# Key products, decay matrices and substitutions of a gated-delta layer moved among its input projections

## The chip, the cores and the metric

The kernel runs on one core of a Trainium2 chip. The time is the device time of one execution in microseconds (us); of several runs the median is given. The engines are TensorE (PE in the profile), VectorE (DVE), ScalarE (ACT), GpSimd (POOL) and SyncE (SP). Each takes its own instructions in a fixed order; a DMA is issued by one of them and moves its data beside them.

## The reference, cut to what matters

Two layers work on 16 meta tokens and 1024 tokens of width 1024, in float32. A layer is a norm, an input projection to 28 blocks of 128 columns, a mixer, an output projection and a feed-forward part. One half of the mixer is a gated delta rule with 4 heads of 128, run forwards and backwards over the sequence:

```python
decay_mat = jnp.exp(jnp.where(incl, G[..., :, None] - G[..., None, :], -jnp.inf))
M = jnp.where(strict, jnp.einsum('bnhid,bnhjd->bnhij', kb, k) * decay_mat, 0.0)
A = M + jnp.eye(CHUNK, dtype=M.dtype)
u = lax.linalg.triangular_solve(A, vb, left_side=True, lower=True, unit_diagonal=True)
w = lax.linalg.triangular_solve(A, kb * jnp.exp(G)[..., None], left_side=True, lower=True, unit_diagonal=True)
attn = jnp.einsum('bnhid,bnhjd->bnhij', q, k) * decay_mat
def step(S, inp):
    v_new = u_c - jnp.einsum('bhcd,bhde->bhce', w_c, S)
    o = jnp.einsum('bhcd,bhde->bhce', qd_c, S) + jnp.einsum('bhij,bhje->bhie', a_c, v_new)
    S = S * gl_c[..., None, None] + jnp.einsum('bhcd,bhce->bhde', kd_c, v_new)
```

k and q are the l2-normalised outputs of a three-tap convolution and a SiLU, G is the running sum of the log decay. The other half of the mixer is a gated short convolution over the remaining columns.

## The kernel before, in words

Activations lie with channels on partitions and the 1040 positions along the free axis. **Dense work** (`dense`, L139) multiplies one block of 128 output columns in fp32r with a split of both operands into a high and a low part: high x high, high x low, low x high (L150, L151, L152), 8 blocks of 128 inputs each, in three column chunks of about 347. ACT writes the high part of a weight (`whi`, L123), POOL the low part (`wlo`, L124); for the first three of the late projections DVE does that (`lov`). An evacuation on DVE multiplies the finished accumulator by the norm (L270). There are three accumulator banks (`pacc`), one bank `pa`, two `pf` and two `pb`.

The 28 projections of a layer go in this order: four k tiles, four q tiles, four v tiles, then 16 for the short convolution and the gate z. Each k, q or v tile gets a convolution (L283, L284) and a SiLU. Sums of squares give the l2 norm (`normalise`); its reciprocal is broadcast through DRAM and multiplied in (L392).

The delta rule goes in 9 chunks (the first of 16 positions, eight of 128) and two directions d. For a chunk the kernel forms K K and K Q products for four heads (L538, L539), loads a row of gate sums (`gr`, from the DRAM tile `gd`), adds a mask on POOL (L550) and takes exponentials on ACT (L548, L552). DVE writes the query side to `aq`, which goes to DRAM (`aqd`; L549, L556), and the key side to P (L560), one tile of 128 x 4160 for each direction. The matrices in P are inverted: first all 32x32 blocks on the diagonal by **substitution**, 31 steps of two vector instructions (L603 multiplies, L604 subtracts), on DVE for d = 0 and on POOL for d = 1; then **merges** on PE to 64x64 and 128x128 blocks (L627 to L653). The chunk of 16 is inverted apart by small instructions on POOL (L572, L573), the meta inversion. The **scan** then takes 9 steps in each direction. A step is a chain: PE (L700), DVE (L703), PE with P (L706), ACT (L710, L713), PE (L717), DVE for the state (L740), beside output products on PE (L731, L732). When both directions have reached a chunk it is finalised (`finalize`, L759 to L771) into O.

The output projection has two halves. The y half, from the short convolution, is dense work without need of the scan. The o half needs O split into a high and a low part (`oh`, `ol`; L827, L828), and these two tiles have the buffers of the two P: they can be written only when the scan has read P for the last time.

What sets the order is a priority list: a scheduler takes, engine by engine, the ready instruction with the lowest number, and the result is a fixed order for each engine. Code written first has lower numbers, unless it sets its own: the merges run at `base-20000+1000d`, the scan at `base-17000` and on, while dense work from the v tiles onwards is put at `base+1000000` (the variable `mmp`) and so fills gaps.

## Time and profile before

| | |
|---|---|
| median of 3 runs | 2680.13 us (2670.06 to 2682.99) |
| the profiled execution | 2667.47 us, span 2665.7 us |
| mean granted clock of TensorE | 0.983 |
| PE busy | 2563.4 us, 96% |
| DVE, ACT, POOL busy | 56%, 39%, 44% |
| DMA | 301.03 MB, mean 113 GB/s |

The profile is one execution; its sums are compared with its own 2667.47 us. A busy PE need not run at full speed: the granted clock is given in a row of its own, in tenths for each fortieth of the span, or as a fraction in a window. "A <- B" in a wait names who waited and for which tile of which line. Line numbers in the profile are those of the kernel before; in the changed kernel most lines after L100 are shifted (L150 to L152 become L152 to L154, the substitution is L506 and L507, the merges to 128x128 are L554 and L556, and the lines of the scan rise by 23).

### The profile page before, as it was taken

To read this page: it belongs to the slowest core of one execution; us is meant where nothing else is said; L and a number is where in the kernel's file an instruction comes from. 1 tells how busy PE (TensorE), PEld (TensorE's weight loads), DVE (VectorE), ACT (ScalarE), POOL (GpSimd) and SP (SyncE) were. 2 spreads that over 40 slices of the span, in tenths; PEclk is the share of its full clock that TensorE was granted. 3 is DMA by queue.
4 is the path that set the end of the run, shared out by engine and by line. 5 is a ranking of instruction groups with operands and counts; after the bars stand their busy time and mean duration, and the time that the engine had idled before them with its cause. 6 is when DMAs were issued, how large, how long until landed. Compare 5 with 4: busy or idle time off the path is not lost. (4 is left out here: it accounts for less than half of the span.)

```text
span 2665.7 us, 43982 instructions
## 1 busy us (share of the span) xinstructions
PE 2563.4 (96%) x17242; PEld 2346.7 (88%) x17242; DVE 1502.8 (56%) x2258; ACT 1032.8 (39%) x1932; POOL 1185.1 (44%) x922
## 2 busy tenths in 40 slices
PE   8998899999999999999999989999989999999997
PEld 7898899998999999999998977898877888887886
DVE  7369713548766566522353688135587766754216
ACT  5466334535333333321244662535343333332224
POOL 4136611224766666533221346112367666663342
PEclk9999889999999999999999999999999999999998
DMA  3246135634312222532222461356332222225321
GB/s 118 98 148 201 49 103 185 193 105 135 104 60 84 80 73 76 198 111 65 76 92 86 125 229 50 125 179 230 99 124 93 68 82 77 87 88 185 93 81 64
DMA packets 163491, 301.03 MB, mean 113 GB/s; under 512 B 20352, under 2 KB 57140, under 8 KB 163284
## 3 DMA queue, kind: packets, MB, share of 16 engines
q1 hardware_dynamic: 163284, 298.23, 34.2%
q8 instruction: 135, 2.21, 0.4%
q14 instruction: 72, 0.59, 0.1%
HBM read 222.99 MB, written 75.18 MB: 112 GB/s over the span
## 5 line engine op out<-in xcount | busy, mean ns | idle before, releaser
L124 POOL TENSOR_TENSOR wlo<-raw,whi 128x512 fp32r<-128x512 f32 x236 | 285.8, 1214 | 927.9 <-ACT whi L123 812.1
L150 PE MATMUL pacc<-a,whi 128*128 128x346 f32 (+2 forms) x1031 | 350.0, 342 | 10.6 <-ACT whi L123 6.1
L152 PE MATMUL pacc<-a,wlo 128*128 128x346 f32 (+2 forms) x1031 | 351.0, 342 | 6.8 <-DVE wlo L124 6.7
L123 ACT ACTIVATE whi<-raw 128x512 fp32r<-128x512 f32 (+2 forms) x264 | 151.7, 578 | 478.9 <-PE pacc L151 300.6
L151 PE MATMUL pacc<-a,whi 128*128 128x346 f32 (+2 forms) x916 | 313.2, 342 | 1.8 <-DVE a L799 1.7
L152 PE MATMUL pacc<-b,wlo 128*128 128x346 f32 (+2 forms) x882 | 303.3, 345 | 8.2 <-DVE wlo L124 8.2
L150 PE MATMUL pacc<-b,whi 128*128 128x346 f32 (+2 forms) x882 | 305.5, 347 | 4.2 <-ACT whi L123 2.1
L151 PE MATMUL pacc<-b,whi 128*128 128x346 f32 (+2 forms) x776 | 268.6, 347 | 0.7 <-DVE b L799 0.6
L150 PEld LDWEIGHTS pacc<-a,whi 128*128 128x128 f32 x1031 | 199.0, 194 | 21.7 <-ACT whi L123 6.5
L152 PEld LDWEIGHTS pacc<-a,wlo 128*128 128x128 f32 x1031 | 199.7, 194 | 16.5 <-DVE wlo L124 8.0
L151 PEld LDWEIGHTS pacc<-a,whi 128*128 128x128 f32 x916 | 177.3, 194 | 10.6 <-DVE a L799 2.0
L150 PEld LDWEIGHTS pacc<-b,whi 128*128 128x128 f32 x882 | 168.2, 191 | 20.1 <-issue 4.2
L152 PEld LDWEIGHTS pacc<-b,wlo 128*128 128x128 f32 x882 | 168.1, 191 | 19.2 <-DVE wlo L124 9.5
L942 POOL TENSOR_TENSOR wlo<-rw,whi 128x512 fp32r<-128x512 f32 x92 | 135.5, 1475 | 71.2 <-ACT whi L941 65.6
L151 PEld LDWEIGHTS pacc<-b,whi 128*128 128x128 f32 x776 | 147.9, 191 | 11.2 <-DVE b L799 1.6
L942 POOL TENSOR_TENSOR a<-rw,a 128x512 fp32r<-128x512 f32 x64 | 107.1, 1676 | 66.5 <-ACT a L941 66.4
L942 POOL TENSOR_TENSOR b<-rw,b 128x512 fp32r<-128x512 f32 x64 | 90.5, 1418 | 83.9 <-ACT b L941 52.3
L804 DVE TENSOR_TENSOR a<-pacc,a 128x346 f32<-128x346 f32 (+2 forms) x116 | 57.7, 500 | 108.3 <-PE pacc L152 107.1
L941 ACT ACTIVATE whi<-rw 128x512 fp32r<-128x512 f32 x92 | 58.0, 632 | 140.1 <-DVE rw L1015 72.5
L804 DVE TENSOR_TENSOR b<-pacc,b 128x512 f32<-128x512 f32 (+1 forms) x88 | 52.6, 599 | 99.2 <-PE pacc L152 98.9
L1011 DVE TENSOR_TENSOR rw<-rw,rw 128x512 f32<-128x512 f32 x44 | 68.5, 1556 | 49.3 <-POOL wlo L942 31.0
L1016 DVE TENSOR_TENSOR rw<-raw,rw 128x512 f32<-128x512 f32 x44 | 95.3, 2165 | 1.2
(822 smaller groups left out, 7504.3 us busy)
## 6 DMA issues: line engine op xcount, KB each, us to landing
raw<-in_w_in SPq DMA_DIRECT2D x112, 256.0 KB
raw<-in_w_gu SPq DMA_DIRECT2D x104, 256.0 KB
rw<-in_w_gu SPq DMA_DIRECT2D x88, 256.0 KB
aqd<-aq SPq DMA_DIRECT2D x32, 512.0 KB
rec<-aqd SPq DMA_DIRECT2D x62, 256.0 KB
rec<-vkd SPq DMA_DIRECT2D x61, 256.0 KB
raw<-in_w_dn SPq DMA_DIRECT2D x60, 256.0 KB
raw<-in_w_out SPq DMA_DIRECT2D x48, 256.0 KB
```

Source lines behind the costliest of these rows:

```text
L123: act(out=hi, in_=raw[:, 0:kk, :], func=AF.Copy)
L124: (tt if lov[0] else ptt)(out=lo, in0=raw[:, 0:kk, :], in1=hi.bitcast(F32), op=ALU.subtract)
L150: mm(ps[:, :n], wh, xh[:, n0:n1], start=(k == 0), stop=False)
L151: mm(ps[:, :n], wh, xl[:, n0:n1], start=False, stop=False)
L152: mm(ps[:, :n], wl, xh[:, n0:n1], start=False, stop=(k == K - 1))
L804: tt(out=hr[m][:, n0:n1], in0=ps, in1=hr[m][:, n0:n1], op=ALU.add)
L941: act(out=hi, in_=src, func=AF.Copy)
L942: ptt(out=lo, in0=src, in1=hi.bitcast(F32), op=ALU.subtract)
L1011: tt(out=s1t, in0=A21, in1=A22, op=ALU.add)
L1016: tt(out=A21, in0=A11, in1=A21, op=ALU.subtract)
```

## The change

The computation stays as it is; its place in the code, two engines and several transfers differ.

- `gates` is built after the third k tile (it was after the seventh of the eight k and q tiles), and its PSUM tiles come from bank `b`, not `a`.
- `normalise` sums squares into four column groups of 260, takes root and reciprocal in place, and issues its stores and broadcast loads from POOL's queue; the broadcast rows land in small tiles, not in a buffer of P.
- `chunks_p`, after the second q tile, does the key half of each chunk: K K products in one bank `b` (priority `base-25000`), mask on POOL, exponentials, P. The decay matrix is also stored to a new DRAM tile `dtd`. Loads and stores go through ACT's queue. The meta inversion gets priority `base+400000`.
- `invert(0)` is called after the q norm, `invert(1)` after the second v tile. Both use DVE and one scratch tile.
- `chunks_a`, after the v tiles, does the query half: K Q products, a second load of the gate rows and a load of the decay matrix (ACT's queue), `aq` and its store.
- The stores of k and v to `vkd` go through ACT's queue; the meta rows of v are stored tile by tile.

The core of the diff (the projection loops, which only move, are left out):

```diff
+    adma = nc.scalar.dma_start
+    qdma = nc.gpsimd.dma_start
...
-        def normalise(dst, l2, r, tag):
+        def normalise(dst, l2, r):
...
-            flat = rnd[r:r + 4].rearrange("a (b c) -> (a b) c", c=40)
-            r104 = row(Y[1] + "f")[0:104, 0:40]
-            dma(r104, flat)
-            nc.vector.reciprocal(out=r104, in_=r104)
-            dma(flat, r104)
-            bc = big(tag)
+            r4 = row(Y[1] + "f")[:, 0:260]
+            act(out=r4, in_=l2[:, 0:260], func=AF.Sqrt, scale=scale, bias=bias)
+            nc.vector.reciprocal(out=r4, in_=r4)
             for h in range(H):
-                dma(bc[:, h, :], rnd[r + h].partition_broadcast(128))
-                tt(out=dst[:, h, :], in0=dst[:, h, :], in1=bc[:, h, :], op=ALU.mult)
+                qdma(rnd[r + h].rearrange("(a c) -> a c", a=4), r4.rearrange("(a b) c -> a b c", b=32)[:, h, :])
+            for h in range(H):
+                bc = c4k("bc")
+                qdma(bc, rnd[r + h].partition_broadcast(128))
+                tt(out=dst[:, h, :], in0=dst[:, h, :], in1=bc, op=ALU.mult)
...
+        def chunks_p():
...
+            for c in range(9):
+                n, s0 = span(c)
+                kk = bank("b").rearrange("p (h i) -> p h i", h=4)
+                def products():
+                    for h in range(H):
+                        mm(kk[0:n, h, 0:n], KTt[:, h, s0:s0 + n], KTt[:, h, s0:s0 + n], start=True, stop=True)
+                at_base(-25000 + 10 * c, products)
+                for d in (dirs0 if c == 0 else (0, 1)):
+                    pn += 1
+                    gr, dt_ = pts[pn % 4], pts[4 + pn % 4]
+                    adma(gr[0:n, :, 0:n], gd[36 * d + 4 * c:36 * d + 4 * c + 4, 0:n].partition_broadcast(n))
+                    ptt(out=gr[0:n, :, 0:n], in0=gr[0:n, :, 0:n], in1=off[0:n, d, 0:n].unsqueeze(1).to_broadcast([n, 4, n]), op=ALU.add)
+                    for h in range(H):
+                        act(out=dt_[0:n, h, 0:n], in_=gr[0:n, h, 0:n], func=AF.Exp, scale=-1.0, bias=negG[0:n, d, c, h:h + 1])
+                    adma(dtd[c, d].rearrange("p (h i) -> p h i", h=4)[0:n, :, 0:n], dt_[0:n, :, 0:n])
+                    for h in range(H):
+                        dst = P0[d][:, h, :] if c == 0 else Pv[d][:, (c - 1) * 4 + h, :]
+                        stt(out=dst, in0=kk[0:n, h, 0:n], scalar=beta[0:n, d, c, h:h + 1], in1=dt_[0:n, h, 0:n], op0=ALU.mult, op1=ALU.mult)
...
+        def chunks_a():
+            for c in range(9):
+                n, s0 = span(c)
+                qk = bank("b").rearrange("p (h i) -> p h i", h=4)
                 for h in range(H):
+                    mm(qk[0:n, h, 0:n], KTt[:, h, s0:s0 + n], QT[:, h, s0:s0 + n], start=True, stop=True)
+                for d in (dirs0 if c == 0 else (0, 1)):
...
+                        eg = t2k("eg")
+                        adma(eg[:, :, 0:n], gd[36 * d + 4 * c:36 * d + 4 * c + 4, 0:n].partition_broadcast(128))
+                        act(out=eg[:, :, 0:n], in_=eg[:, :, 0:n], func=AF.Exp, scale=-1.0)
+                        tt(out=qd0 if c == 0 else qd, in0=QT[:, :, s0:s0 + n], in1=eg[:, :, 0:n], op=ALU.mult)
+                    dt_ = t2k("dt")
+                    adma(dt_[0:n, :, 0:n], dtd[c, d].rearrange("p (h i) -> p h i", h=4)[0:n, :, 0:n])
+                    tt(out=at0[d] if c == 0 else at, in0=qk[0:n, :, 0:n], in1=dt_[0:n, :, 0:n], op=ALU.mult)
+                    if c > 0:
+                        dma(aqd[c, d].rearrange("p a b -> p (a b)"), aq[:, 0:1024])
...
-                itt(out=Tm[:, i0:i1, a0:a1], in0=W[:, i0:i1, j:j + 1].to_broadcast(sh), in1=Xi[:, j:j + 1, a0:a1].to_broadcast(sh), op=ALU.mult)
-                itt(out=Xi[:, i0:i1, a0:a1], in0=Xi[:, i0:i1, a0:a1], in1=Tm[:, i0:i1, a0:a1], op=ALU.subtract)
+                tt(out=Tm[:, i0:i1, a0:a1], in0=W[:, i0:i1, j:j + 1].to_broadcast(sh), in1=Xi[:, j:j + 1, a0:a1].to_broadcast(sh), op=ALU.mult)
+                tt(out=Xi[:, i0:i1, a0:a1], in0=Xi[:, i0:i1, a0:a1], in1=Tm[:, i0:i1, a0:a1], op=ALU.subtract)
...
+            if pos == 2:
+                beta, g, negG, negE, gl, bkd = gates()
+            if pos == 3:
+                normalise(KTt, l2, 4)
+            if pos == 5:
+                for c in range(9):
+                    k_out(c)
+                chunks_p()
+        normalise(QT, l2, 0)
+        invert(0)
...
+            if i == 1:
+                invert(1)
+        chunks_a()
```

Three places show what the scheduler makes of it in layer 0. The second direction's substitution is the first: POOL before, where L550 is the mask of a chunk, L502 a product of the short convolution, and `b_418` the scratch tile of d = 1.

```order
L550 TENSOR_TENSOR ptm_3158<-ptm_3158,off 128x512
L502 TENSOR_TENSOR b_231_1841<-b_231_1841,b_232_1845 128x1040
L603 TENSOR_TENSOR b_418_3604<-b_418_3604 128x31
L604 TENSOR_TENSOR b_418_3604<-b_418_3604 128x31
L603 TENSOR_TENSOR b_418_3604<-b_418_3604 128x30x2
L604 TENSOR_TENSOR b_418_3604<-b_418_3604 128x30x2
```

And DVE now, where L126 is the low part of a weight, L272 an evacuation and `b_220` the scratch tile of d = 1:

```order
L272 TENSOR_TENSOR b_351_3060<-pacc_3073,rstd_81 128x348
L500 STREAM_TRANSPOSE b_220_2087<-b_220_2087 128x1024
L506 TENSOR_TENSOR b_220_2087<-b_220_2087 128x31
L272 TENSOR_TENSOR b_351_3060<-pacc_3099,rstd_81 128x346
L507 TENSOR_TENSOR b_220_2087<-b_220_2087 128x31
L506 TENSOR_TENSOR b_220_2087<-b_220_2087 128x30x2
L507 TENSOR_TENSOR b_220_2087<-b_220_2087 128x30x2
L506 TENSOR_TENSOR b_220_2087<-b_220_2087 128x29x3
L507 TENSOR_TENSOR b_220_2087<-b_220_2087 128x29x3
L506 TENSOR_TENSOR b_220_2087<-b_220_2087 128x28x4
L507 TENSOR_TENSOR b_220_2087<-b_220_2087 128x28x4
L126 TENSOR_TENSOR wlo_3161<-raw_3162,whi_3160 128x512
```

The substitution of d = 1 has moved from POOL to DVE and shares that queue with evacuations and low parts of weights.

The second place is PE at the merges of 64x64 blocks, L651 and L653 before (`pf`, `pb` are banks, `P_3149` and `P_3150` the matrices of d = 0 and d = 1, L627 a 32x32 merge; `x8` means eight instructions):

```order
L152 MATMUL pacc_2470<-a_1_72,wlo_2407 128x346
L627 MATMUL pb_4106<-b_418_3604,P_3150 32x32 x3
L653 MATMUL pf_3878<-P_3149,b_417_3603 64x64 x8
L651 MATMUL pf_3897<-b_417_3603,P_3149 64x64 x8
L627 MATMUL pb_4106<-b_418_3604,P_3150 32x32 x13
L653 MATMUL pf_3898<-P_3149,b_417_3603 64x64 x8
L651 MATMUL pf_3917<-b_417_3603,P_3149 64x64 x8
L627 MATMUL pb_4106<-b_418_3604,P_3150 32x32 x13
L653 MATMUL pf_3918<-P_3149,b_417_3603 64x64 x8
L653 MATMUL pf_3937<-P_3149,b_417_3603 64x64 x8
L627 MATMUL pb_4106<-b_418_3604,P_3150 32x32 x3
L150 MATMUL pacc_2470<-a_1_72,whi_2406 128x346
```

The same merges of d = 0 on PE now, as L554 and L556 (`P_1002` is the matrix of d = 0):

```order
L154 MATMUL pacc_3004<-a_3_74,wlo_2973 128x346
L556 MATMUL pf_1807<-P_1002,b_179_1539 64x64 x8
L554 MATMUL pf_1826<-b_179_1539,P_1002 64x64 x8
L152 MATMUL pacc_3004<-a_3_74,whi_2972 128x346
L153 MATMUL pacc_3004<-a_5_76,whi_2972 128x346
L154 MATMUL pacc_3004<-a_3_74,wlo_2973 128x346
L152 MATMUL pacc_3004<-a_3_74,whi_2972 128x346
L153 MATMUL pacc_3004<-a_6_77,whi_2972 128x346
```

The merges of the two directions stood together without dense work between them; now those of one direction stand alone, two groups at a time between runs of dense matmuls.

The third place is PE at the last read of P. Before, L706 is that read in the last step but one of d = 1, L770 a transpose of a finalise, and the rest is the dense work of an input projection, with the y half still to come:

```order
L151 MATMUL pacc_3123<-a_2_73,whi_3059 128x346
L706 MATMUL pb_4286<-vv_4282,P_3150 128x128 x4
L770 MATMUL pa_4944<-ident,b3f_4287 128x128 x4
L152 MATMUL pacc_3123<-a_1_72,wlo_3060 128x346
L150 MATMUL pacc_3123<-a_1_72,whi_3059 128x346
L151 MATMUL pacc_3123<-a_2_73,whi_3059 128x346
```

Now L729 is that read, L740 the state product, L754 and L755 the output products, L793 the transpose; the row after the last of these belongs to the next step, and the next dense rows are those of the o half:

```order
L153 MATMUL pacc_5614<-a3f_5229,whi_5580 128x346
L154 MATMUL pacc_5614<-a_521_5214,wlo_5581 128x346
L729 MATMUL pb_4373<-vv_4369,P_1003 128x128 x4
L793 MATMUL pa_5031<-ident,b3f_4374 128x128 x4
L740 MATMUL pb_4372<-vv_4369,rec_4364 128x128 x4
L754 MATMUL pb_4373<-S_4367,rec_4364 128x128
L755 MATMUL pb_4373<-vv_4369,rec_4364 128x128
```

The last read of P has moved from the last input projections to behind the last matmul of the y half.

More of the change, by code (lines that the diff above doesn't have):

```diff
@@ L658, in trunk @@
             at_prio(sub_end)
+        for pos, i in enumerate((4, 5, 6, 7, 0, 1, 2, 3)):
+            hh = pos % 4
+            if hh == 0:
+                l2, squares = None, []
+            t = trow()
+            late = pos < (2, 1)[l]
+            inproj(i, to_row_late(t) if late else to_row(t), pfirst if l == 0 and pos == 1 else None)
+            if late:
+                tt(out=t, in0=t, in1=rstd, op=ALU.mult)
+            dst = (QT if i < 4 else KTt)[:, hh, :]
+            conv(t, dst, P_CV + 3 * i)
+            act(out=dst, in_=dst, func=AF.Silu)
+            act(out=t, in_=dst, func=AF.Square)
+            squares.append((hh, t))
+            if l > 0 or pos > 0:
+                if l2 is None:
+                    l2 = bank("f")
+                for (q, sq_) in squares:
+                    for j, (n0, n1) in enumerate([(260 * j, 260 * j + 260) for j in range(4)]):
+                        mm(l2[32 * j:32 * j + 32, :n1 - n0], sel[:, 3 - q:35 - q], sq_[:, n0:n1], start=(q == 0), stop=(q == 3), skip_group_check=True)
+                squares = []
+            if pos == 2:
[6 more added lines that the diff above has]
+                chunks_p()
@@ new lines, in trunk, with z_tile, low @@
+        normalise(QT, l2, 0)
+        invert(0)
+        mmp[0] = base + 1000000
+        def z_tile(m):
+            t = trow()
+            inproj(12 + m, to_row(t), chunks=ochunks)
+            t = t[:, o0:L]
+            act(out=t, in_=t, func=AF.Silu)
+            nc.gpsimd.tensor_scalar(out=t, in0=t, scalar1=pcol(P_DN), scalar2=1.0, op0=ALU.mult, op1=ALU.mult)
+            dma(szd[m][:, o0:L], t)
+        def low(f):
+            here = tc.cur_priority
+            at_prio(mmp[0])
+            f()
+            mmp[0] = tc.cur_priority
+            at_prio(here)
@@ new lines, in v_store @@
+        def v_store(i, v):
+            for c0 in (0, 1, 5):
+                ps = pa()
+                if c0 == 0:
+                    low(lambda: nc.tensor.transpose(ps[0:16, 0:128], v[:, 0:16], ident))
+                    vm = wp.tile([128, WK, 128], F32, tag="raw", bufs=2, name=nm("vm"))[0:16, 0, :]
+                    nc.vector.tensor_copy(vm, ps[0:16, 0:128])
+                    dma(vkd[0, 0:16, 0, i * 128:(i + 1) * 128], vm)
+                else:
+                    vt = v[:, 16 + 128 * (c0 - 1):16 + 128 * (c0 + 3)]
+                    for c in range(4):
+                        low(lambda: nc.tensor.transpose(ps[:, c * 128:(c + 1) * 128], vt[:, 128 * c:128 * c + 128], ident))
+                    act(out=vt, in_=ps, func=AF.Copy)
+                    adma(vkd[c0:c0 + 4, :, 0, i * 128:(i + 1) * 128].rearrange("c p e -> p c e"), vt.rearrange("p (c e) -> p c e", c=4))
@@ new lines, in trunk, with sc_tile, times, f @@
+        v = None
+        for i in range(4):
+            t = trow()
+            inproj(8 + i, to_row(t))
+            if i > 0:
+                v_store(i - 1, v)
+            v = trow() if i % 2 == 0 else row(Y[1] + "f")
+            conv(t, v, P_CV + 3 * (8 + i))
+            act(out=v, in_=v, func=AF.Silu)
+            if i == 1:
+                invert(1)
+        chunks_a()
+        def sc_tile(i, then=None):
+            t0 = trow()
+            inproj(16 + 3 * i, to_row(t0))
+            if then is not None:
+                then()
+            ptt(out=t0, in0=t0, in1=rstd, op=ALU.mult)
+            def times(t):
+                def f(ps, n0, n1):
+                    tt(out=t[:, n0:n1], in0=ps, in1=t[:, n0:n1], op=ALU.mult)
+                return f
+            inproj(17 + 3 * i, times(t0))
+            t2 = trow()
+            conv(t0, t2, P_SC + 3 * i)
+            if i < 3:
+                t1 = trow()
+                inproj(18 + 3 * i, to_row(t1), chunks=ochunks)
+                ptt(out=t2[:, o0:L], in0=t2[:, o0:L], in1=t1[:, o0:L], op=ALU.mult)
+                dma(yd[i][:, o0:L], t2[:, o0:L])
+            else:
+                ptt(out=t2, in0=t2, in1=rstd, op=ALU.mult)
+                inproj(18 + 3 * i, times(t2), chunks=ochunks)
+            return t2
@@ L661, in trunk @@
+        y3 = None
+        for j, q in enumerate((0, 4, 1, 5, 6, 2, 7, 3)):
+            lov[0] = j < 3
+            if q < 4:
+                y3 = sc_tile(q, (lambda: v_store(3, v)) if j == 0 else None)
+            else:
+                z_tile(q - 4)
+        lov[0] = False
+        mmp[0] = None
+        top = tc.cur_priority
         rec = sb.tile([128, 4 * L], F32, tag=Y[0][2], name=nm("rec"))
```

215 lines of the change are left out of this document (45 added, 170 removed).

## The prediction

> **What bounds the kernel now.** I read the page first (busy shares and the clock row), then windows of 40 us over the part of each layer that the change touches, then the waits of PE there, then the groups of the instructions that move. Three rows of the page:
>
> ```profile
> PE 2563.4 (96%) x17242; PEld 2346.7 (88%) x17242; DVE 1502.8 (56%) x2258; ACT 1032.8 (39%) x1932; POOL 1185.1 (44%) x922
> PEclk9999889999999999999999999999999999999998
> q1 hardware_dynamic: 163284, 298.23, 34.2%
> ```
>
> PE is the bound at 96%, so a change that adds no matmul can only win back PE's idle time and time at a lowered clock, and can lose by adding to either. The windows show where both lie: busy us of PE, PEld, DVE, ACT and POOL, then the granted clock, the share of the DMA engines and GB/s. The first five rows are layer 0, the last four layer 1.
>
> ```profile
> 160.00:200.00 40.00, 37.15 (x255) 34.60 (x254) 28.28 (x64) 26.29 (x55) 20.30 (x33) 1.00 0.68 216
> 200.00:240.00 40.00, 34.28 (x230) 33.51 (x230) 37.55 (x83) 26.67 (x61) 31.89 (x48) 0.96 0.68 225
> 240.00:280.00 40.00, 35.59 (x210) 34.44 (x209) 36.22 (x65) 15.12 (x19) 21.68 (x28) 0.96 0.38 129
> 280.00:320.00 40.00, 34.43 (x335) 33.10 (x334) 31.66 (x50) 11.40 (x15) 28.62 (x43) 0.91 0.14 47
> 320.00:360.00 40.00, 38.65 (x579) 35.90 (x578) 8.85 (x11) 17.82 (x27) 3.52 (x3) 0.67 0.12 40
> ...
> 1520.00:1560.00 40.00, 34.01 (x232) 31.86 (x231) 32.05 (x80) 29.72 (x64) 26.21 (x41) 1.00 0.71 226
> 1560.00:1600.00 40.00, 35.34 (x176) 30.79 (x175) 38.10 (x78) 23.46 (x45) 15.54 (x16) 0.92 0.60 205
> 1600.00:1640.00 40.00, 34.08 (x177) 31.14 (x176) 38.73 (x58) 6.28 (x9) 34.76 (x46) 0.93 0.16 49
> 1640.00:1680.00 40.00, 38.99 (x635) 31.21 (x633) 19.89 (x27) 22.15 (x31) 13.92 (x18) 0.99 0.17 59
> ```
>
> In layer 0, PE idles 2.9 + 5.7 + 4.4 + 5.6 + 1.4 = 19.9 us, with DVE nearly full; and 0.04, 0.04, 0.09 and 0.33 of four windows of 40 us are lost to the clock, 20.0 us. In layer 1 it is 6.0 + 4.7 + 5.9 + 1.0 = 17.6 us idle and 6.4 us of clock. So 64 us in all can be won here. The large clock loss is the stretch of the 64x64 merges, where PE counts as fully busy at half speed; the last row is from the first scan steps, among dense work again:
>
> ```profile
> 340.00:345.00 5.00, 5.00 (x31) 4.08 (x30) 0.52 (x1) 0.59 (x1) 0.00 (x0) 0.50 0.00 0
> 350.00:355.00 5.00, 5.00 (x70) 4.82 (x68) 0.00 (x0) 1.18 (x2) 0.00 (x0) 0.50 0.00 0
> ...
> 375.00:380.00 5.00, 5.00 (x57) 4.48 (x54) 1.12 (x4) 1.78 (x3) 0.00 (x0) 1.00 0.15 50
> ```
>
> The largest waits of PE in 160 to 365 us name DVE and ACT:
>
> ```profile
> PE pacc L152 <- DVE wlo L124: 6.7, 3, 4.2
> PE pa L463 <- ACT b L471: 4.4, 1, 4.4
> PE pb L538 <- DVE P L560: 2.9, 3, 1.3
> ```
>
> No DMA is among them, although the DMA share is 0.68 there.
>
> **The substitutions.** Both directions ran side by side, one on DVE, one on POOL (busy us, mean ns):
>
> ```profile
> L603 DVE TENSOR_TENSOR b<-b 128x31 f32<-128x31 f32 (+15 forms) x31 | 17.0, 547 | 0.8
> L604 DVE TENSOR_TENSOR b<-b 128x31 f32<-128x31 f32 (+15 forms) x31 | 16.8, 542 | 0.7
> L604 POOL TENSOR_TENSOR b<-b 128x31 f32<-128x31 f32 (+15 forms) x31 | 19.7, 637 | 2.2
> L603 POOL TENSOR_TENSOR b<-b 128x31 f32<-128x31 f32 (+15 forms) x31 | 17.9, 576 | 9.2 <-DVE b L593 7.1
> ...
> L603 DVE TENSOR_TENSOR b<-b 128x112 f32<-128x112 f32 x2 | 0.5, 268 | 0.0
> L603 DVE TENSOR_TENSOR b<-b 128x255 f32<-128x255 f32 x2 | 1.6, 824 | 0.0
> L603 DVE TENSOR_TENSOR b<-b 128x256 f32<-128x256 f32 x1 | 0.4, 424 | 0.0
> ```
>
> One substitution costs DVE 33.8 us beside a busy POOL. The single 128x256 instruction took 424 ns where 128x255 took 824: with 268 ns at 112 elements, a quiet POOL gives 147 ns + 1.08 ns an element, and the 31 sizes sum to 5456 elements, so 2 x (31 x 0.147 + 5456 x 0.00108) = 20.9 us. The Trainium skill ("SBUF — State Buffer", two separate sides) says that DVE with two inputs in SBUF and GpSimd hold a shared port pair in turn, whole instruction by whole instruction. The pair of rows agrees; by that rule alone the sum would take the quiet price throughout.
>
> So DVE gets 20.9 to 33.8 us more, POOL 37.6 us less, and the first substitution gets up to 12.9 us cheaper. They now lie apart, each between input projections. A projection of three chunks has 72 matmuls, 0.16 us apart (the first and the tenth of a run without other work):
>
> ```profile
> 391.07 0.32 PE L152 MATMUL pacc<-a,wlo 128*128 128x346 f32 x1
> ...
> 392.51 0.32 PE L152 MATMUL pacc<-a,wlo 128*128 128x346 f32 x1
> ```
>
> That is 11.5 us of PE. Counting DVE's new order at the group means (estimates from before's rows), three successive projections around the first substitution carry 27.9, 16.1 and 16.9 us of DVE, together 61 at the contended price and about 50 at the quiet one. PE has 35 us there, and the three accumulators let DVE lag by one projection, 11 us. PE then stalls 61 - 46 = 15 us, or 4. POOL still runs the meta inversion and the low splits there, so neither end holds alone; the slow half of its work is gone, so I take 8. Around the second substitution four projections carry 58.9 (or 47) us against 46 + 11: 2 or 0, I take 1. Other waits stay as in 160 to 200 us: 3. Clock: layer 1 lost 6.4 us with 17.6 idle, 0.36 for each idle us; on 9 us it is 3. In the new order the 64x64 merges stand between dense matmuls, so I drop the 13 us at half clock; if that cover fails, they return. The front then costs 8 + 1 + 3 + 3 = 15 us a layer: **layer 0 gains 39.9 - 15 = 25, layer 1 24.0 - 15 = 9**.
>
> **What is late next: the scan.** Query products follow the v tiles, so the first scan step moves from 21.3 projections' worth of dense work to 25.5, while that filler (28 projections and the y half of w_out) ends at 32.0 as before. Before, the last finalise stood at 29.7, 2.3 projections or 26 us short of the end. Now the last read of P stands exactly at the end of the filler in layer 0; in layer 1 about two steps of both directions and two more of direction 1 stand behind it. The o half of w_out cannot fill this: its operands oh and ol lie in P's own buffers. The parts of a step:
>
> ```profile
> 375.78 1.16 PE L700 MATMUL pf<-S,b 128*128 128x128 f32 x8
> ...
> L703 DVE SCALAR_TENSOR_TENSOR vv<-pf,negE,rec 128x128 f32<-128x128 f32 x32 | 9.0, 343 | 12.3 <-PE pf L700 11.3 <-issue 1.0
> L710 ACT ACTIVATE vv<-pf,bkd 128x128 f32<-128x128 f32 (+1 forms) x32 | 9.2, 364 | 13.0 <-PE pf L706 13.0
> L740 DVE SCALAR_TENSOR_TENSOR S<-S,gl,pf 128x128 f32<-128x128 f32 x28 | 9.5, 345 | 20.4 <-PE pf L731 19.2
> L828 DVE TENSOR_TENSOR o<-b,o 128x260 fp32r<-128x260 f32 x12 | 6.1, 557 | 1.1 <-ACT o L827 0.8 <-PE pb L706 0.3
> L827 ACT ACTIVATE o<-b 128x260 fp32r<-128x260 f32 x12 | 4.2, 431 | 0.0
> ```
>
> A lone step is 3 x 1.16 on PE + 4 x (0.343 + 0.364 + 0.345) = 7.7 us, in which PE has 20 products (two records each), 5.8 us; 2 to 4 us idle a step, less where two directions interleave. The first four splits of oh and ol before dense work resumes add 4 x 0.56, about 2. Layer 0: one and a half lone steps and the split, 5 us. Layer 1: two double steps, two lone ones and the split, 10. The bounds are 0 (the filler is late too) and 22 (each of those steps all idle off PE). **Together -15.**
>
> **Transfers.** Decay matrices are stored and loaded again, the gate rows are loaded twice. The kinds before, the fullest window, and three rows of the norm:
>
> ```profile
> aqd<-aq SPq DMA_DIRECT2D x32, 512.0 KB
> ptm<-gd SPq DMA_DIRECT2D x32, 256.0 KB
> P<-rnd SPq DMA_DIRECT2D x16, 520.0 KB
> ...
> 195.00:200.00 5.00, 4.65 (x35) 4.35 (x34) 5.00 (x12) 3.10 (x8) 4.45 (x10) 1.00 0.95 293
> L392 DVE TENSOR_TENSOR b<-b,P 128x1040 f32<-128x1040 f32 x4 | 5.9, 1506 | 1.8 <-DMA P<-rnd 1.8
> L387 DVE RECIPROCAL b3f<-b3f 104x40 f32<-104x40 f32 x1 | 0.4, 403 | 0.3 <-DMA b3f<-rnd 0.3
> L182 DVE RECIPROCAL rstd<-rstd 128x346 f32<-128x346 f32 (+1 forms) x3 | 6.7, 2281 | 0.7 <-ACT rstd L181 0.7
> ```
>
> The key stretch moves 16 x (256 + 256) KB with weights and the broadcast loads of the norm, 11.5 MB: 39 us at 293 GB/s, against 1.8 projections and 36 products, 31 us. The query stretch moves 16 x (256 + 256 + 512) KB and weights, 18 MB: 61 us against 49. So 0 to 20 us a layer. Before, 160 to 240 us moved 17.6 MB in 80 us and no DMA was waited for, and the scan uses the query chunks over more time than they take; I take 2.5 a layer, near the low end: **-5**. These transfers go from SP to ACT's and POOL's queues. On ACT, a load that waits for a buffer stands ahead of the splits of weights; in the new order such buffers are freed by DVE at 5 to 9 us a projection, which is slack. SP keeps the weights, the aq stores and the scan's loads. The Trainium skill ("DMA: Bandwidth & Descriptors", issuing engines are not separate DMA queues) says that spreading over engines only saves issue time. The page's single large queue row cannot show it; by that rule the two stretches need the 61 and 39 us whoever issues.
>
> **The norm, the gates, the meta inversion.** Reciprocals of 104x40 become 128x260 in place, between 0.4 and 2.3 us (the nearest rows, 104x40 and 128x346, the latter nearer), less two round trips through DRAM; four mults at 1.5 us stay. Nothing waits for them but the 1.8 us of L392. I price them at 0 to -2 and take 0. Gates change a PSUM bank and place: 0. K and v stores wait on ACT behind their own copies: 0. The meta operations stay on POOL and end long before the scan: 0.
>
> **Sum.** 25 + 9 - 15 - 5 = 14 us gained. The profiled execution took 2667.5 us (span 2665.7), so 2653 by its own time; the median of the runs shown is 2680.1, 12.7 above it, and 2680.1 - 14 = **2666 us** is the forecast. 0.5%, or 13 us, is about what can be told from no change.
>
> **Rivals.** (a) POOL quiet enough that both substitutions hide, and the tail covered: front 6 a layer, tail 8, transfers 0: 64 - 12 - 8 = 44 gained, 2636. For it: 424 against 824 ns. Against it: DVE's 27.9 us beside one projection. (b) Slower: the tail at half clock. It has some 38 products in layer 0 and 132 in layer 1 with no dense matmul between, 170 x 0.29 = 49 us; at clock 0.50, as in 340 to 355 us, they take 49 us more: 2680 - 14 + 49 = 2715. It makes the kernel slower once over 27 of the 49 are lost. Against it: the scan's products at 375 us ran at 1.00, among dense ones. The Trainium skill ("TensorE: Matmul & The Clock Gate", what's actually happening) has half rate after about 3.4 us idle. Here the lone chain never idles so long by my reckoning, so by that rule (b) is out; but the rows at 340 and 350 show half speed with PE at 5.00, so the trace does not bear the rule out. (c) Transfers bound: 20 instead of 2.5 us a layer, 2666 + 35 = 2701. For it: 0.95 at 293 GB/s. Against it: no wait for a DMA in the list. (d) POOL issues the norm's loads, two of them behind a dozen meta operations and a low split that waits for ACT; DVE, in order, stands at the mult with evictions behind it. Against it: 1.8 us for four loads before. At worst each of the two stands behind two waits like the longest above, 4.2 and 4.4: 17 us a layer, 2666 + 34 = 2700; from 14 a layer, 2694, the kernel is slower. [...]
>
> **Chances.** Forecast 0.42 (half of it over the 0.5% bound), (a) 0.20, (b) 0.13, (c) 0.13, (d) 0.12. Faster by over 0.5%: 0.21 + 0.20 = 0.41; slower: (b), (c) and a part of (d), 0.30; the rest, 0.29, within. The forecast's own range is 2650 to 2682. To leave out no more than 0.2 the range takes in (a), (c) and (d) and ends just short of (b): 2630 to 2710.
>
> **What the profile will show.** Right: 64x64 merges at clock near 1.00; no window with DVE at 36 or more over 100 us; substitution means below 450 ns; PE waits of 9 us or so for DVE in the front; 5 and 10 us idle ahead of the o half of w_out. Wrong: PE waits for L389 or L484 behind DMAs, DMA share at 0.95 over the query stretch, or a low clock at the end of the scan.

## The result, and the profile after

The changed kernel took 2701.95 us (median of 6 runs, 2695.47 to 2709.92) beside 2681.56 us for the kernel before on the same chip. The ratio is **1.0097, 95% interval 1.0075 to 1.0120**: some 26 us slower, where 14 us of gain were forecast. (The ratios are estimates of their own, not quotients of the medians, which here is 1.0076, 20 us.) On another chip, beside the later experiments, it was 1.0099 (1.0081 to 1.0117). The profiled execution took 2699.28 us, 31.8 more than the profiled one of before, which with 2667.47 us lay 14 us under the median of its kernel.

The page of the changed kernel, engines, clock and the largest DMA queue:

```profile
PE 2569.5 (95%) x17274; PEld 2351.5 (87%) x17274; DVE 1534.6 (57%) x2347; ACT 1042.9 (39%) x1937; POOL 1123.0 (42%) x830
PEclk9988999999999999999999899999899999999999
q1 hardware_dynamic: 143196, 272.57, 30.7%
```

PE is counted busy 6 us more, DVE 32 us more, POOL 62 less. Of the 31.8 us, 25.7 are idle time of PE (128.0 against 102.3) and 6.1 are busy time, in which matmuls at a lowered clock are counted with their full length. Below, the idle time of a window and the time that its mean clock is short of 1.00 are added up, as in the prediction; where the clock is low while PE idles, the same microsecond is counted twice, so these sums are larger than the time that is lost. The dip of the clock row has moved from the fifth and sixth slice to the third and fourth, and the same front in layer 1 and the end of its scan show as eights further on (23rd and 29th slice). The windows of the front in the changed kernel (columns as before: PE, PEld, DVE, ACT, POOL, clock, DMA share, GB/s), layer 0 and then layer 1:

```profile
80.00:120.00 40.00, 34.37 (x209) 31.57 (x207) 20.15 (x18) 22.46 (x37) 19.78 (x21) 0.91 0.45 141
120.00:160.00 40.00, 37.30 (x250) 34.43 (x248) 27.36 (x77) 28.14 (x67) 17.73 (x13) 0.96 0.55 191
160.00:200.00 40.00, 31.10 (x175) 28.27 (x175) 31.67 (x54) 25.66 (x32) 22.55 (x38) 0.83 0.46 149
200.00:240.00 40.00, 32.47 (x327) 30.53 (x326) 29.73 (x59) 22.60 (x28) 14.27 (x37) 0.87 0.28 78
240.00:280.00 40.00, 39.53 (x446) 37.67 (x445) 12.56 (x21) 17.75 (x27) 2.39 (x1) 0.91 0.23 67
...
1440.00:1480.00 40.00, 36.79 (x236) 33.58 (x236) 27.23 (x46) 23.42 (x39) 17.96 (x19) 0.96 0.54 167
1480.00:1520.00 40.00, 34.43 (x237) 31.76 (x235) 26.93 (x67) 31.30 (x63) 18.53 (x21) 1.00 0.57 190
1520.00:1560.00 40.00, 29.72 (x162) 28.43 (x162) 30.85 (x55) 15.98 (x19) 21.31 (x33) 0.79 0.46 142
1560.00:1600.00 40.00, 38.27 (x514) 36.21 (x515) 20.15 (x36) 19.39 (x29) 2.38 (x1) 0.91 0.25 74
```

Layer 0 loses 25.2 us idle and 20.8 us to the clock, 46 in all; layer 1 20.8 + 13.6 = 34. The kernel before lost 40 and 24, over later windows. In 160 to 240 us DVE is busy 61 of 80 us, so over 40 us it does not look full; in steps of 5 us it is. Four of them:

```profile
175.00:180.00 5.00, 2.71 (x18) 2.22 (x16) 4.72 (x13) 2.42 (x3) 3.75 (x8) 1.00 0.27 97
180.00:185.00 5.00, 2.23 (x8) 1.43 (x8) 4.75 (x11) 2.36 (x3) 4.30 (x10) 0.56 0.80 249
185.00:190.00 5.00, 2.14 (x8) 1.70 (x8) 5.00 (x4) 4.61 (x6) 3.98 (x5) 0.50 0.78 241
...
215.00:220.00 5.00, 1.13 (x5) 0.71 (x4) 4.03 (x15) 0.51 (x1) 3.13 (x12) 0.81 0.00 1
```

From 170 to 220 us, the stretch of a substitution, DVE is busy 46.7 of 50 us, and 11.8 of PE's 16.4 idle us lie there.

The tail of layer 1, where the scan ends and the o half begins:

```profile
1840.00:1880.00 40.00, 38.18 (x219) 32.86 (x218) 14.29 (x33) 12.95 (x39) 6.25 (x5) 1.00 0.41 125
1880.00:1920.00 40.00, 31.89 (x232) 29.34 (x231) 21.86 (x59) 21.41 (x92) 0.38 (x1) 0.89 0.45 146
1920.00:1960.00 40.00, 33.51 (x240) 32.35 (x239) 29.45 (x58) 21.00 (x56) 12.20 (x8) 0.84 0.39 116
```

PE's waits there name the scan's chain and then the splits of O:

```profile
PE pf L729 <- DVE a3f L782: 3.4, 1, 3.4
PE pa L793 <- DVE a3f L791: 3.1, 1, 3.1
PE pacc L152 <- ACT o L850: 2.2, 1, 2.2
```

Over 1840 to 2040 us, idle and clock come to 25.5 + 13.6 = 39 us; in the kernel before the same five windows lose 15.7. That is 23 us more; the front adds some 5 in layer 0 and 8 in layer 1, the end of layer 0's scan 7 (555 to 600 us), and other places give part of it back. Edges of windows cut the work at different places, and a second execution of the changed kernel loses 35 us in the tail, not 39, so these sums are good to a few us.

### The profile page after: what moved, and what is told of

The parts are those of the page before. It is cut to its first block, busy times and chain, and to the rows that moved or that the text cites. A ratio compares the mean times of both kernels' runs of the same rounds, so it can differ in the third digit from the quotient of the medians.

```text
span 2697.5 us, 44121 instructions
## 1 busy us (share of the span) xinstructions
PE 2569.5 (95%) x17274; PEld 2351.5 (87%) x17274; DVE 1534.6 (57%) x2347; ACT 1042.9 (39%) x1937; POOL 1123.0 (42%) x830
## 4 chain that ended last, share of the span: by engine, by line
PE 71%; DVE 12%; ACT 5%; issue 4%; DMA 4%; POOL 4%; ACTq 0%; SPq 0%; POOLq 0%; DVEq 0%
PE pacc L152 10%; PE pacc L154 10%; PE pacc L153 10%; PE pacc L982 3%; PE pacc L983 3%; PE pacc L984 3%; PE pf L152 2%; PE pf L153 2%; PE pf L154 2%; PE pf L982 2%; PE pf L984 2%; PE pb L982 2%; PE pf L983 2%; PE pb L984 2%; PE pb L983 2%
## 5 line engine op out<-in xcount | busy, mean ns | idle before, releaser
L126 POOL TENSOR_TENSOR wlo<-raw,whi 128x512 fp32r<-128x512 f32 x236 | 284.9, 1210 | 867.6 <-ACT whi L125 695.6
L152 PEld LDWEIGHTS pacc<-a,whi 128*128 128x128 f32 x1031 | 198.7, 193 | 26.8 <-ACT whi L125 11.8
```

What stands on the lines that cost most here:

```text
L126: (tt if lov[0] else ptt)(out=lo, in0=raw[:, 0:kk, :], in1=hi.bitcast(F32), op=ALU.subtract)
L152: mm(ps[:, :n], wh, xh[:, n0:n1], start=(k == 0), stop=False)
```

## The experiments

Five theories were on the table. A: in the front the transposes of k and v, in one bank `pa`, wait for copies that stand in full queues. B: DVE has too much with both substitutions. C: the tail, because the query products and with them the scan come late. D: what POOL does slows DVE, so that only a quiet POOL makes the two substitutions cheap. E: SP, in order, stands behind the stores of the meta inversion, which now come early, and weights behind it come late. Each ratio is to the kernel before on the same chip. The changed kernel and the first experiment on the kernel before were each run a second time (1.0099; 0.9938, 0.9915 to 0.9960).

**1. The copy of v's meta rows on ACT (theory A).** In the changed kernel:

```diff
-                    nc.vector.tensor_copy(vm, ps[0:16, 0:128])
+                    act(out=vm, in_=ps[0:16, 0:128], func=AF.Copy)
```

> The meta rows of v are copied out of PSUM by ACT instead of DVE (L625), nothing else; the changed kernel stands at 1.0097 times the kernel before. Theory A (the front loses through transposes of k and v: one bank, whose copies stand in crowded queues): the waits of PE for L625 (5.3 us in layer 0, 7.8 in layer 1) go, with some of the low clock behind them, so 8 to 18 us are won, ratio 1.003 to 1.007. Theory B (DVE's load from two substitutions): PE waits for the next thing DVE owes, ratio 1.008 to 1.011. Theory C (the scan's tail alone) expects no change, 1.0097.

Measured: 1.0032 (1.0012 to 1.0052). It is 0.65% or 17 us faster than the changed kernel, and the number lies in A's range, but it was not won where A has it: over 80 to 320 us of layer 0, idle and clock lose 47.2 us, and 46.0 before the edit. The wait of `pa` only changed the engine it names:

```profile
PE pacc L152 <- DVE b L272: 3.7, 1, 3.7
PE pa L630 <- ACT vm L625: 3.3, 3, 2.6
```

The front of layer 1 (1440 to 1600 us) loses 31.8 us, not 34.4, and the tail of layer 1 28.9, not 39: most of what the windows show is won there, with query products that start 8.5 us earlier in layer 1. Why they do was not followed.

**2. The norm's transfers on SP's queue.** In the changed kernel `qdma` becomes `dma` in the two places of `normalise`.

> The sixteen DMAs of the two norms of a layer are issued by SP again, not by POOL. Theory D (POOL's issues and its masks hold up DVE's instructions: L286 took 4.67 us beside them and one substitution step 2.33): these long instructions go, the idle of PE at 100 to 110 us (5.7 us) and part of that at 180 to 190 go, in both layers, 10 to 16 us won, ratio 1.003 to 1.006. Theory A and C: within 3 us of the changed kernel, 1.0085 to 1.011.

Measured: 0.9988 (0.9968 to 1.0007), that is 1.09% or 29 us faster than the changed kernel. Two lines of the changed kernel, POOL's wait and one group of the convolution on DVE (75 to 240 us):

```profile
POOL rnd L385 <- DVE b3f L383: 8.6, 1, 8.6
...
L286 DVE SCALAR_TENSOR_TENSOR b<-b,par,b 128x1039 f32<-128x1039 f32 x7 | 13.4, 1916 | 0.1
```

The same group with the norm's transfers on SP:

```profile
L286 DVE SCALAR_TENSOR_TENSOR b<-b,par,b 128x1039 f32<-128x1039 f32 x7 | 9.0, 1292 | 0.1
```

POOL stood 8.6 us behind the reciprocal of the q norm, with the low parts of weights and the meta inversion queued behind it. At the k norm it ran three masks in a row right behind its stores, from 97.9 to 102.3 us, and the one convolution beside them took 4.67 us where most of its group take 1.3: 3.4 of the 4.4 us between the two rows. With SP the front of layer 0 (80 to 280 us) loses 38 us, not 46, and the tail of layer 1 loses 24.8, not 39; the query products start 17 us earlier in layer 0 and 25 us in layer 1. Which of POOL's delays this comes from is not separated by this run.

**3. The meta transfers on POOL's queue (theory E).** In the changed kernel the five transfers of the meta inversion use `qdma`.

> The five small DMAs of each meta inversion are issued by POOL, not by SP. Theory E (SP stands before the store L461 until POOL has finished, and weights wait behind it: a load issued at 219.4 us when POOL ended at 219.0): PE's waits for L125 (4.3 us in layer 0) go and 3 to 8 us are won, ratio 1.0065 to 1.0085. Theories A to D: no change, 1.0085 to 1.011.

Measured: 1.0064 (1.0037 to 1.0091), 0.33% or 9 us below the changed kernel, with intervals that overlap. Two waits of the changed kernel in 160 to 240 us, of SP's queue and of ACT:

```profile
SPq L461 <- POOL mt L460: 13.4, 1, 13.4
...
ACT whi L125 <- DMA raw<-in_w_in: 6.1, 2, 5.7
```

The store of the meta result holds SP for 13.4 us, the weights behind it land late and the split waits: E's mechanism is there. The front of layer 0 (80 to 320 us) loses 36 us in this run, not 46, but in the time of the kernel the gain can hardly be told from none.

**4. The query products in bank `f` (theory C).** In the changed kernel:

```diff
-                qk = bank("b").rearrange("p (h i) -> p h i", h=4)
+                qk = bank("f").rearrange("p (h i) -> p h i", h=4)
```

> The query products use PSUM bank f instead of b, nothing else; in the new order they run from 14.4 projections of dense work, not 20.6, and the last read of P stands at 29.6 instead of 32.0 in layer 0 and 89.0 instead of past the end 89.8 in layer 1. Theory C (the tail): idle and low clock ahead of the o half, 7 us in layer 0 and 19 in layer 1, go: 20 to 26 us won, ratio 1.000 to 1.002. Theory B (DVE's load): the query work falls into the crowd of the second substitution, 12 to 17 projections, and up to 15 us a layer come back as waits there: ratio 1.003 to 1.010.

Measured: 0.9985 (0.9968 to 1.0001): 1.12% or 30 us faster by one word. The query products' own line, number, min/median/max ns and the times of the first and last of them; the changed kernel, layers 0 and 1:

```profile
L472 PE MATMUL pb<-b,b x72: 176/275/377, 362.5 to 409.0; 128*128 128x128 f32 x64, 128*16 128x16 f32 x8
...
L472 PE MATMUL pb<-a,a x72: 176/275/377, 1715.0 to 1760.4; 128*128 128x128 f32 x64, 128*16 128x16 f32 x8
```

And in bank `f`:

```profile
L472 PE MATMUL pf<-b,b x72: 176/275/378, 272.2 to 320.0; 128*128 128x128 f32 x64, 128*16 128x16 f32 x8
...
L472 PE MATMUL pf<-a,a x72: 176/275/377, 1605.4 to 1650.7; 128*128 128x128 f32 x64, 128*16 128x16 f32 x8
```

They run 90 and 110 us earlier. Bank `b` is taken in program order, and the second direction's merges hold it (`pb`), in layer 0 from 316.0 to 358.8 us; the query products, which in bank `f` start at 272.2, stood behind them. The scan then ends under the filler, and the tail of layer 1 is full:

```profile
1840.00:1880.00 40.00, 40.00 (x262) 35.78 (x262) 23.92 (x57) 16.15 (x63) 5.34 (x4) 1.00 0.49 163
1880.00:1920.00 40.00, 40.00 (x268) 36.34 (x267) 25.72 (x54) 20.99 (x69) 9.52 (x7) 1.00 0.30 94
1920.00:1960.00 40.00, 37.41 (x298) 36.00 (x297) 36.07 (x56) 22.89 (x39) 22.40 (x15) 1.00 0.48 153
```

1840 to 2040 us lose 12.9 us in place of 39. The front is as it was (45 us in layer 0).

**5. Edits 2, 3 and 4 together.**

> Norm DMAs back on SP, meta DMAs on POOL, query products in bank f, all three. If the three causes are apart (tail 26 us, POOL's issues 16 us in the fronts, SP's wait 9 us), 40 to 50 us are won on the changed kernel: ratio 0.991 to 0.995. If the norm edit won mostly by an earlier scan, so that it shares its gain with the bank, 30 to 38 us: ratio 0.9955 to 0.9985.

Measured: 0.9950 (0.9931 to 0.9970), 1.47% or 39 us below the changed kernel. The three alone add up to 2.5%: 2 and 4 both win in the tail of layer 1, where alone they take 14 and 26 us off the 39.

**6. Edits 2 and 4 without 3.** This tells the meta transfers apart.

> The changed kernel with the query products in bank f and the norm's transfers on SP's queue; the meta transfers stay on SP, which is all that tells it from the run with three edits (ratio 0.995 to the kernel before). Theory M: SP's wait behind the meta stores costs as much here as in the changed kernel, 9 us, so this one stands at 0.998, some 9 us above the run with three edits. Rival: with SP carrying the norm's transfers and POOL free of them, POOL's queue with the meta transfers is what holds the masks up, as it did at the old place (0.54% there), so that this one is 8 to 14 us below the run with three edits: 0.990 to 0.992.

Measured: 0.9958 (0.9942 to 0.9973), between the two and 0.08% from run 5: neither theory. Beside the other two edits the meta transfers are worth nothing that can be told, though SP waits 11.3 us behind the same store here. The two edits undo the slowdown, but not the front: it still loses 40 us in layer 0 (80 to 320 us) and 28 in layer 1 (1440 to 1600 us), while the tail of layer 1 loses 15.7, as before the change.

**7. Without v's transposes (theory A again).** On top of run 5.

> As the three together, and v's transposes with their copies are left out (v is stored as it stands, its values then being in the wrong places): 36 transposes a layer, at four in 0.6 us 5 us of PE. Theory A (PE's order holds transposes that wait for copies in crowded queues): beside these 11 us, 15 to 30 us of idle and low clock in the two fronts go, ratio 0.010 to 0.015 below that of the three together. Theory B (the fronts wait for DVE and ACT whatever stands there): 8 to 14 us, 0.003 to 0.005 below.

Measured: 0.9911 (0.9884 to 0.9938), 0.39% or 10 us below run 5: PE's own work that is left out (PE is busy 10.4 us less in the profile, which is 10.9 us shorter). The waits for `pa` are gone, and in layer 0 PE waits for weights instead:

```profile
PE pacc L152 <- ACT whi L125: 11.1, 3, 7.6
```

The front of layer 1 (1440 to 1600 us) loses 21.6 us here and 35.2 in run 5, but other places give that back. With runs 1 and 7, A is not borne out: taking away the waits that the list named did not shorten the kernel by more than the work left out.

**8. The second substitution back on POOL (theories B and D).** On top of run 5, `(tt, ptt)[d]` in place of `tt`.

> As the three together, but the second substitution is on POOL again. Theory B (DVE's load): DVE loses about 21 us a layer in the second crowd, 4 to 15 us won, ratio 0.0015 to 0.0055 below that of the three together. Theory D (POOL beside DVE is what costs): low splits of weights wait behind 37 us of POOL and DVE slows, 5 to 15 us lost, 0.002 to 0.0055 above.

Measured: 1.0007 (0.9988 to 1.0026), 0.57% slower than run 5, and the front of layer 0 (80 to 320 us) loses 44.5 us, not 35.8. The groups in layer 0:

```profile
L507 POOL TENSOR_TENSOR b<-b 128x31 f32<-128x31 f32 (+15 forms) x31 | 22.2, 715 | 2.4
L506 POOL TENSOR_TENSOR b<-b 128x31 f32<-128x31 f32 (+15 forms) x31 | 19.6, 633 | 15.8 <-DVE b L500 13.5
L507 DVE TENSOR_TENSOR b<-b 128x31 f32<-128x31 f32 (+15 forms) x31 | 15.6, 503 | 0.8
L506 DVE TENSOR_TENSOR b<-b 128x31 f32<-128x31 f32 (+15 forms) x31 | 11.7, 378 | 0.7
```

**9. The kernel before with both substitutions on DVE, nothing else.**

```diff
-            itt = (tt, ptt)[d]
+            itt = tt
```

> The kernel before with one part of the change alone: both substitutions on DVE, at their old place. DVE has 36 to 39 us of 40 there in two to three windows of a layer. Theory B: 21 to 34 us more on DVE a layer appear almost whole as PE's waits, 20 to 60 us lost, ratio 1.008 to 1.022. Theory D: the quiet POOL gives 13 us back and low splits come sooner: ratio 0.998 to 1.005.

Measured: **0.9924 (0.9899 to 0.9950)**, again 0.9938. Both substitutions, 62 steps to a line:

```profile
L604 DVE TENSOR_TENSOR b<-b 128x31 f32<-128x31 f32 (+15 forms) x62 | 22.3, 387 | 0.2
L603 DVE TENSOR_TENSOR b<-b 128x31 f32<-128x31 f32 (+15 forms) x62 | 22.0, 385 | 0.2
```

44.3 us for two, 22.2 each, where one took 33.8 beside POOL. DVE does twice the substitutions for 10 us more, and B falls at this place.

**10. The same with the low parts of the late weights off DVE and on POOL.** `lov[0] = False` besides. (`lov` is set for three turns of the loop, and these hold seven projections: 14 instructions of 128x512 in layer 0.)

> The kernel before with both substitutions on DVE and all low splits of weights on POOL (in it the first seven late projections have them on DVE, 10.7 us in layer 0). Theory B: DVE, at 39.9 and 39.5 us of 40 in two windows, gets 11 us back a layer, 6 to 16 us won, 0.9865 to 0.990. Theory D: the same work on POOL beside DVE's substitutions slows both, 0 to 12 us lost, 0.9924 to 0.997.

Measured: 0.9998 (0.9981 to 1.0015). DVE has less to do, POOL more, and the gain is gone:

```profile
L603 DVE TENSOR_TENSOR b<-b 128x31 f32<-128x31 f32 (+15 forms) x62 | 28.6, 492 | 0.2
L604 DVE TENSOR_TENSOR b<-b 128x31 f32<-128x31 f32 (+15 forms) x62 | 24.8, 429 | 0.1
```

53.4 us for the same 124 instructions. That bears D out on the price: DVE's time for a two-input instruction in SBUF depends on what POOL does. The Trainium skill ("SBUF — State Buffer", two separate sides) has the two engines hold a shared port pair in turn; 44.3 and 53.4 us agree. How these 9 us become 16 to 20 us of the kernel was not followed: in 150 to 400 us PE waits 7.2 us for evacuations, 1.8 in run 9.

**11. Small transfers at the old place.** Three runs on the kernel before. The norm's transfers on POOL's queue:

> The kernel before with another part of the change alone: the norm's seven DMAs of each of the two tensors are issued by POOL, not SP. Theory D (POOL's issues stand against DVE and behind POOL's own queue): 3 to 15 us lost, ratio 1.001 to 1.006, seen in longer DVE instructions or in waits for L392. The rival, that the gain of putting these DMAs back in the changed kernel came from the order alone: 0.9985 to 1.001.

Measured: 1.0003 (0.9988 to 1.0018). Run 9 with the meta transfers on POOL's queue:

> The kernel before with both substitutions on DVE and the meta DMAs on POOL's queue. If the meta DMAs are what cost 15 us in the two queue moves together: 0.996 to 0.999. If the stores of k and v were it: as the substitutions alone, 0.991 to 0.9945.

Measured: 0.9992 (0.9979 to 1.0005), 0.54% worse than run 9 beside it. Run 9 with k and v stores on ACT's queue and the meta transfers on POOL's:

> The kernel before with both substitutions on DVE, k's and v's stores on ACT's queue and the meta DMAs on POOL's. Theory E (SP stands behind the meta store): 3 to 9 us below the substitutions alone, ratio 0.989 to 0.9913. Its rival, that at the old place SP has slack there: 0.9915 to 0.9945.

Measured: 0.9982 (0.9966 to 0.9998). One window of run 9, the merges in layer 0:

```profile
320.00:360.00 40.00, 39.92 (x747) 37.31 (x744) 3.69 (x8) 23.10 (x36) 3.65 (x3) 0.83 0.25 80
```

And with the meta transfers on POOL's queue:

```profile
320.00:360.00 40.00, 38.09 (x668) 35.18 (x662) 6.71 (x11) 20.73 (x31) 7.11 (x6) 0.69 0.16 56
```

The merges lose 18.8 us to the clock over 320 to 400 us in place of 6.8, and come later: the first of 64x64 starts at 342.1 us, not 335.1, the last at 384.3, not 369.7. What delays them is not shown. POOL's last mask is only 2 us later (239.7 and 237.7 us) and the last write to P not at all (246.2 and 246.0). So the edit that seemed to win 0.33% in the changed kernel costs 0.54% here, and the norm's, worth 1.09% there, is worth nothing here.

**12. The stores of k and v.** Run 5 with these stores on SP's queue, and run 9 with them on ACT's:

> As the three together, and k's and v's stores on SP again. If these stores cost in the changed kernel too: 5 to 12 us below the three together, 0.9905 to 0.993. If not: 0.9935 to 0.997.

> The kernel before with both substitutions on DVE and k's and v's stores on ACT's queue. If these stores are what cost (an issue of 0.3 to 0.6 us stands in ACT's queue ahead of splits and copies): 0.996 to 0.999. If the meta DMAs were it: 0.991 to 0.9945.

Measured: 0.9942 (0.9924 to 0.9959) beside 0.9950, and **0.9911 (0.9884 to 0.9937)** beside 0.9938. The edit itself can't be told from nothing in either. The second has the lowest ratio of the kernels that leave nothing out, 2650.89 us beside 2678.02 of the kernel before on the same chip, but by these intervals it is no faster than run 9 alone.

**13. That kernel with the changed form of the norm.** Root and reciprocal in place of 128x260, rows in small tiles, transfers on SP:

> The kernel before with both substitutions on DVE, the k and v stores on ACT's queue, and the changed kernel's norm (root and reciprocal in place of 128x260, broadcast rows in small tiles) with its transfers on SP. Theory: the form of the norm is worth nothing at the old place, since only 1.8 us waited for its loads: the ratio stays at that of the run without it, 0.988 to 0.994. Rival N: the two round trips through DRAM that it saves bring the first scan nearer, and the buffers of P are free earlier, so some 5 to 8 us more: 0.985 to 0.988. Rival R: the reciprocals of 128x260 on DVE stand before the convolutions and cost more than the trips: 0.995 or above.

Measured: 0.9952 (0.9934 to 0.9970). Against run 12 (0.9911) that is 0.41% or 11 us worse, against run 9 (0.9938 and 0.9924) 0.14 to 0.28%; the intervals overlap in each case. It points to rival R and does not show it. The reciprocals take 1.78 us each, as in the changed kernel, where the small ones took 0.40, and DVE waits for the roots first:

```profile
L383 DVE RECIPROCAL b3f<-b3f 128x260 f32<-128x260 f32 x2 | 3.6, 1778 | 4.7 <-ACT b3f L382 4.7
```

These are some 7 us a layer more on DVE's queue. The mults wait 8.0 us for their broadcast rows, 6.8 in run 12, so the round trips that are saved do not show there. The two kernels ran on different occasions, each beside its own runs of the kernel before, and whether the 7 us reach PE was not followed.

**What the parts come to.** Both substitutions on DVE: -0.7%. The other parts of the change: +1.7% (some 45 us). Of these, the bank of the query products and the queue of the norm's transfers hold 1.39% (1.0097 against 0.9958, run 6), the form of the norm 0.1 to 0.4%, if it is real. What is left of the change then, the early key half, the second loads and the stores of the decay matrices, is the difference between run 6 (0.9958) and run 13 (0.9952), on one chip: nothing that can be told. So with the bank and the queue mended, the early placement neither won nor lost.

## Why the prediction was wrong

**The front, 15 us a layer: this step failed.** Measured 46 and 34. Its idle time was put at 8 + 1 + 3 = 12 us a layer, and from where the prediction looked that was not far off: from 160 us on PE idles 16.9 us in layer 0, from 1520 us on 12.0 in layer 1. Two other terms failed. The clock was put at 3 us, 0.36 for each idle us, a rate taken from layer 1 of the kernel before; in the same windows it is 15.6 and 12.0, about one for each idle us. And the projections ahead were put at nothing, though chunk work of the key half and the norm had moved among the k and q tiles: 80 to 160 us, where the kernel before loses 1.6 us, lose 13.5 now, and 1440 to 1520 us 10.4 in place of 2.5.

The backlog of DVE on which the step was built is there, but not alone. Nine kinds of wait sum to 25 us, and the longest single one is 3.3 us. The first four of them, from 75 to 285 us of the changed kernel:

```profile
PE pa L630 <- DVE vm L625: 5.3, 2, 3.2
PE pacc L152 <- ACT whi L125: 4.3, 2, 2.2
PE pacc L152 <- DVE b L272: 3.3, 1, 3.3
PE pa L397 <- ACT kt L399: 3.1, 2, 2.1
```

The waits for DVE make some 9 us, as forecast. The others name ACT, which itself stood up to 6.0 us behind DVE's substitution (L284 at 219.5 us). That DVE is full there does not show that its load set the time: with the second substitution back on POOL (run 8) the front loses more. Which chain sets the front stays open; in run 6, where the slowdown is undone, it still loses 40 and 28 us.

**The merges at clock near 1.00: right where dense work stands beside them, but no gain in sum**, since the clock was lost earlier: 160 to 240 us lose 12 us to it, 240 to 280 us 3.6. A run of dense matmuls at 248.1 to 252.3 us, right ahead of the first of 64x64, is at half speed too (0.49 us each, 0.32 after it).

**One substitution 20.9 to 33.8 us: right**, 25.3 in the changed kernel (50.5 for two), 22.2 with a quieter POOL. Rival (a) had the mechanism, and run 9 shows it worth 0.7% by itself. It was priced only together with the rest.

**The tail, 5 and 10 us: right in the idle time, short by the clock and by the cause.** 555 to 600 us hold 3.3 idle and 3.6 clock in layer 0; 1875 to 1925 us hold 10.5 idle and 7.0 clock in layer 1. But the sum over 1840 to 2040 us is 23 worse than before, with the norm and the feed-forward's start behind it. The prediction took the late query products as given ("Query products follow the v tiles"); it was the bank that held them, 90 and 110 us, and with bank `f` the tail loses 12.9 us, less than before the change. That wait was not seen, and the bank of `gates` was priced at nothing without a run to take it apart.

**Rival (b), the tail at half clock, partly.** The scan's lone chain did fall to 0.59 and 0.50. What the reckoning denied is there, a long idle stretch within a step, and the next eight products of that shape took 2.08 us in place of 1.16:

```profile
1901.68 2.08 PE L729 MATMUL pf<-vv,P 128*128 128x128 f32 x8 [3.39 <-DVE a3f L782]
```

The Trainium skill ("TensorE: Matmul & The Clock Gate", what's actually happening) has half rate after about 3.4 us idle; this row agrees. The front shows that less is enough: from 175 to 190 us no wait is longer than 2.13 us, PE is busy 7.1 of 15 us, and the clock falls to 0.50.

**Transfers, 5 us, and rival (c): no wait of PE names a transfer.** PE is full through the query stretch, 370 to 420 us, at 338 GB/s and more.

**The norm at 0: wrong on the queue, open on the form.** The queue of its transfers is rival (d), "POOL issues the norm's loads": right on the queue, POOL's wait is 8.6 us, and undone it gives 29 us against the 34 that (d) was given. That the sizes are near is luck: (d) had DVE stand at the mults, which waited 0.9 us in layer 0, and half of the gain lies in the tail. It had a chance of 0.12. The form may cost 4 to 11 us (run 13); each reciprocal takes 1.78 us, within the bound of 2.3, but the wait of DVE for the roots, 4.7 us in layer 0 of run 13, was not counted.

**K and v stores at 0: right within the measurement (run 12). The meta operations at 0: open.** Their transfers moved alone give 9 us, with intervals that overlap (run 3), beside the other two edits nothing (runs 5 and 6).

**The signs.** The signs of being right came true and did not tell: the means of the substitution are 401 and 415 ns, no 40 us window of the fronts has DVE at 36, PE waits some 9 us for DVE, and 3.3 and 10.5 us idle stand ahead of the o half. Of the signs of being wrong, the DMA share of 0.95 came without a cost to PE, and the low clock at the end of the scan came with one.

## What to carry to other kernels

A change that moves work in a full, in-order schedule is not priced by the busy time of the fullest engine: look for what each moved instruction waits for on its queue, and which bank or buffer it takes in program order, since one word for a bank was worth 30 us here. Do the part that has a clear mechanism alone: both substitutions on DVE won 0.7% where the whole change lost 1%. The price of moving a small transfer to another queue does not carry over: the same five transfers cost 14 us at one place and nothing that can be told at another. And look for idle time in steps of 5 us: over 40 us an engine that is full for the length of the wait looks half free.
